# A gated group norm whose mean square and root are computed on all 128 partitions over the whole block, in place of column sums, a root on four columns, and diagonals

## The chip, the cores and the metric

The kernel runs on one core of one Trainium2 chip. The metric is the device time of one execution in microseconds. TensorE is called PE, VectorE DVE, ScalarE ACT, GpSimd POOL, and SyncE, which issues most of the transfers, SP.

## The reference

One layer of a hybrid decoder trunk over T = 2112 tokens (2048 of a prompt, 64 of a sample group) of width 1024, all in float32. Three token mixers (a Mamba-2 scan, a convolution module, a causal pooling) are projected from the same normed input, gated and merged. What the change touches is the end of the Mamba branch:

```python
def rmsnorm(x, w):
    xf = x.astype(jnp.float32)
    y = xf * lax.rsqrt(jnp.mean(xf * xf, axis=-1, keepdims=True) + EPS)
    return (y * w.astype(jnp.float32)).astype(x.dtype)

def mamba_branch(z, xbc, dt_raw, ...):
    ...
    y, h_new = ssd_scan(xs, dt, a_log, bm, cm, h0)
    y = (y + d_skip[:, None].astype(y.dtype) * xs).reshape(bsz, L, D_SSM)
    yg = (y * jax.nn.silu(z)).reshape(bsz, L, SSM_GROUPS, D_SSM // SSM_GROUPS)
    yg = rmsnorm(yg, jnp.ones((D_SSM // SSM_GROUPS,), jnp.float32)).reshape(bsz, L, D_SSM)
    return yg * norm_w.astype(yg.dtype), new_buf, h_new
```

So the 1024 channels of `y * silu(z)` are divided by the root mean square of their group of 512 (two groups), one root for each token and group. `z` is a product of the normed input with 1024 columns of the input projection.

## The kernel before

Activations lie transposed, channels on the partitions and tokens along the free axis. The tokens are cut into five blocks, `TB`: 512, 512, 512, 256 and 320. Every float32 product of the projections is made of float16 halves: `mm3` issues, for each of the 8 slices of the contraction, three matmuls (24 in all, each of one block's tokens) that add into one PSUM tile `mm`, of which there are three in turn (`mmt`). PE's instructions keep the order in which the program writes them. The other engines' instructions are put in order by the framework's scheduler, which simulates the kernel; an engine then takes its instructions strictly in that order.

Work that goes beside the products is put into a list, `side`. After each matmul of `mm3` the list's clock moves on by n / 2400 us, and a step of the list whose time has come is written at that place. `z_norm` below is such a step: it comes 9.0 us of that clock behind its block.

The stage of the change is the z stage (lines 1234 to 1287 before): for each of the two channel groups `g`, and in it for the blocks in the order 256, 320, 512, 512, 512, `z_in` does four times (`cc`), for 128 channels each:

- SP loads `yg` (the scan's result, from DRAM, L1247 and L1249; eight buffers) and `xs` (L1252; two buffers), and DVE makes `yg + d * xs` in `yg` (L1253);
- PE makes the product of z, 24 matmuls (L365, tile `mm`);
- ACT takes its silu out of PSUM into `sz` (L1258; one buffer), which gives the `mm` tile back, and DVE multiplies `yg` by it (L1259);
- ACT squares `yg`, for the first `cc` into `sacc` (L1261; one buffer), for the others into `sz` (L1263), and DVE adds `sz` to `sacc` (L1264).

Then `z_norm`: for each 128 tokens a matmul of a block of `sacc` with one column of ones gives the sums over the partitions as a column (L1272, tile `pvz`, 128 x 1). `rstd_of` (L179 to L186) makes the inverse root of up to four such columns on DVE, by the integer first guess and three Newton steps, twelve instructions on 128 x 4. 7.0 us later `bcast_steps` spreads the root over the partitions again: for each 128 tokens DVE makes a diagonal (L197) and PE multiplies ones by it (L199, tile `rBz`). DVE multiplies the four `yg` by `rBz` (L1280), ACT and DVE make from each the two float16 halves `ya` (L1281, L1282), which later products of the output projection read.

Weights of later products are converted during the stage too: ACT (L228, L247) and DVE (L251, 128 x 1024, two in a row), with a small product for the scale (L136 on PE into an `mm` tile, read by L138 on DVE).

Of the kernel before, what the change touches and what calls it, by code (L numbers as in the profile page):

```python
# [11 lines left out]
F32 = mybir.dt.float32  # L12
F16 = mybir.dt.float16
BF16 = mybir.dt.bfloat16
I32 = mybir.dt.int32
AF = mybir.ActivationFunctionType
ALU = mybir.AluOpType
# [4 lines left out]
P = 128  # L22
# [9 lines left out]
EPS = 1e-6  # L32
# [10 lines left out]
def tiles_of(n):  # L43

    return [min(o, n - P) for o in range(0, n, P)]
# [7 lines left out]
def trunk_body(tc, I, O):  # L53
    nc = tc.nc
    V, S, G, PE, DMA = nc.vector, nc.scalar, nc.gpsimd, nc.tensor, nc.sync
    MUL, ADD, SUB, MAX = ALU.mult, ALU.add, ALU.subtract, ALU.max
# [36 lines left out]
    ident, tri, ones = cst[:, C_ID:C_ID + P], cst[:, C_TRI:C_TRI + P], cst[:, C_ONE:C_ONE + P]  # L93
# [77 lines left out]
    def rstd_of(ss, n, cnt, eng, name):  # L171

        r = ss.shape[0]

        def sm(nm, dt=F32):
            return smp.tile([P, 4], dt, name=nm, tag=f"rs_{nm}", bufs=4)[:r, :n]

        v, i1, y, a, b = sm("rv"), sm("ri", I32), sm("ry"), sm("ra"), sm("rb")
        V.tensor_scalar(v, ss, 1.0 / cnt, EPS, op0=MUL, op1=ADD)  # L179
        V.tensor_scalar(i1, v.bitcast(I32), 1, None, op0=ALU.logical_shift_right)  # L180
        V.tensor_scalar(y.bitcast(I32), i1, -1.0, float(0x5F3759DF), op0=MUL, op1=ADD)
        for it in range(3):
            eng.tensor_tensor(a, y, y, op=MUL)
            eng.scalar_tensor_tensor(b, a, -0.5, v, op0=MUL, op1=MUL)
            y2 = sm(f"ry{it}")
            eng.scalar_tensor_tensor(y2, b, 1.5, y, op0=ADD, op1=MUL)  # L186
            y = y2
        return y

    def bcast_steps(ps, cols, offs, pace=0.64):  # L190

        dgs = []
        for i, o in enumerate(offs):
            while len(dgs) < min(i + 3, len(offs)):
                q = len(dgs)
                dgs.append(smp.tile([P, P], F32, name="diag", tag="diag", bufs=3))
                V.tensor_scalar(dgs[q], ident, cols[:, q:q + 1], None, op0=MUL)  # L197
            yield pace
            PE.matmul(ps[:, o:o + P], ones, dgs[i], start=True, stop=True)  # L199
# [159 lines left out]
    side, wside = Side(), Side()  # L359
# [102 lines left out]
    start = tc.manual_schedule(engines={mybir.EngineType.DVE, mybir.EngineType.Activation, mybir.EngineType.SP})  # L462
# [766 lines left out]
    pps = pool("pps", 2, space=PSUM)  # L1229
    zps = pool("zps", 2, space=PSUM)  # L1230

    Z_GAPS = (9.0, 7.0)

    def z_in(g, bi, zw):

        t0, n = TB[bi]
        pn = PN[bi]
        sacc = zp.tile([P, 512], F32, name="sacc", tag="sacc")[:, :n]
        yg = []
        for cc in range(4):  # L1240
            k = 4 * g + cc

            o = n * (cc % 2) if 2 * n <= 512 else 0
            if o == 0:
                yt = zp.tile([P, 512], F32, name="yg", tag="yg", bufs=8)
            yk = yt[:, o:o + n]
            DMA.dma_start(out=yk[:, :pn].rearrange("p (i t) -> p i t", t=P), in_=y_d[t0 // P:(t0 + pn) // P, :, k].rearrange("i p t -> p i t"))  # L1247
            if pn < n:
                DMA.dma_start(out=yk[:, pn:], in_=y_d[NC, :, k, :TS])  # L1249
            yg.append(yk)  # L1250
            xs = zp.tile([P, 512], F32, name="xs", tag="xs", bufs=2)[:, :n]
            DMA.dma_start(out=xs, in_=xbc_d[k, :, t0:t0 + n])  # L1252
            V.scalar_tensor_tensor(yk, xs, dsk[:, k:k + 1], yk, op0=MUL, op1=ADD)  # L1253
            wz, iz = zw[cc // 2]
            pz = mmt(n)
            mm3(pz, wz, (cc % 2) * P, hT[bi], n)
            sz = zp.tile([P, 512], F32, name="sz", tag="sz", bufs=1)[:, :n]
            S.activation(sz, pz, AF.Silu, scale=iz)  # L1258
            V.tensor_tensor(yk, yk, sz, op=MUL)  # L1259
            if cc == 0:  # L1260
                S.activation(sacc, yk, AF.Square)  # L1261
            else:
                S.activation(sz, yk, AF.Square)  # L1263
                V.tensor_tensor(sacc, sacc, sz, op=ADD)  # L1264
        side.add(z_norm(g, bi, yg, sacc), Z_GAPS[0])

    def z_norm(g, bi, yg, sacc):
        n = TB[bi][1]
        offs = tiles_of(n)
        pv = zps.tile([P, 4], F32, name="pvz", tag="pvz", bufs=1)  # L1270
        for i, o in enumerate(offs):
            PE.matmul(pv[:, i:i + 1], sacc[:, o:o + P], ones[:, 0:1], start=True, stop=True)  # L1272
            yield 0.64
        rs = rstd_of(pv[:, :len(offs)], len(offs), 512, V, "z")
        yield Z_GAPS[1]
        rB = zps.tile([P, 512], F32, name="rBz", tag="rBz", bufs=2)
        yield from bcast_steps(rB, rs, offs)
        for cc in range(4):
            k = 4 * g + cc
            V.tensor_tensor(yg[cc], yg[cc], rB[:, :n], op=MUL)  # L1280
            S.activation(ya[bi][:, 0, k], yg[cc], AF.Copy, scale=snws[:, k:k + 1])  # L1281
            V.scalar_tensor_tensor(ya[bi][:, 1, k], yg[cc], snws[:, k:k + 1], ya[bi][:, 0, k], op0=MUL, op1=SUB)  # L1282

# [247 lines left out]
```

## Time and profile before

| | us |
|---|---|
| median of 3 runs | 2228.59 |
| lowest and highest | 2225.47, 2231.59 |
| profiled execution | 2221.09 |
| its span in the trace | 2219.0 |
| PE busy in it | 2148.2 (97%) |
| DVE busy | 1369.9 (62%) |
| ACT busy | 908.4 (41%) |
| POOL busy | 255.9 (12%) |

The profile comes from one execution, the 2221.09 us; the 2.1 us by which that is longer than the span lie outside it. Start times in the trace count from the span's start. "Busy" is the time in which the engine has an instruction in work; for PE overlapping matmuls count once. A float32 matmul leaves two records in the trace. [...]

### The profile page before, as it was taken

To read this page: it belongs to the slowest core of one execution; us is meant where nothing else is said; L and a number is where in the kernel's file an instruction comes from. 1 tells how busy PE (TensorE), PEld (TensorE's weight loads), DVE (VectorE), ACT (ScalarE), POOL (GpSimd) and SP (SyncE) were. 2 spreads that over 40 slices of the span, in tenths; PEclk is the share of its full clock that TensorE was granted. 3 is DMA by queue.
4 is the path that set the end of the run, shared out by engine and by line. 5 is a ranking of instruction groups with operands and counts; after the bars stand their busy time and mean duration, and the time that the engine had idled before them with its cause. 6 is when DMAs were issued, how large, how long until landed. Compare 5 with 4: busy or idle time off the path is not lost.

```text
span 2219.0 us, 33878 instructions
## 1 busy us (share of the span) xinstructions
PE 2148.2 (97%) x13188; PEld 1275.5 (57%) x13188; DVE 1369.9 (62%) x2414; ACT 908.4 (41%) x1647; POOL 255.9 (12%) x579
## 2 busy tenths in 40 slices
PE   5999999999999999999999999999999999999998
PEld 3565555555555565545555555556645555557886
DVE  6689888884777786889954443436676332233544
ACT  6431444458666564154343232224444222232222
POOL 0010111111111111132210011100000000001222
PEclk9999999999999999999999999999999999999999
DMA  7332221226665554452323233334241222236321
GB/s 267 119 88 74 74 88 69 88 90 208 171 152 167 166 151 149 157 180 84 111 84 99 73 114 116 116 107 143 83 130 62 90 91 66 74 109 208 115 101 44
DMA packets 203505, 259.57 MB, mean 117 GB/s; under 512 B 51409, under 2 KB 142161, under 8 KB 203345
## 3 DMA queue, kind: packets, MB, share of 16 engines
q1 hardware_dynamic: 184848, 218.89, 31.8%
q0 software_dynamic: 6896, 22.30, 2.9%
q10 hardware_dynamic: 11600, 16.22, 2.1%
q8 instruction: 103, 1.69, 0.3%
q14 instruction: 58, 0.47, 0.1%
HBM read 179.06 MB, written 78.30 MB: 116 GB/s over the span
## 4 chain that ended last, share of the span: by engine, by line
PE 67%; DVE 16%; DMA 6%; ACT 5%; issue 4%; POOL 1%; SPq 0%; DVEq 0%; POOLq 0%; ACTq 0%
PE mm L365 51%; DVE acc L665 6%; DVE ct L729 4%; PE po L1390 2%; PE po L1391 2%; PE po L1392 2%; PE y L843 2%; DMA R<-acT_d 1%; DVE w L251 1%; DMA xs<-xbc_d 1%; ACT w L247 1%; PE off L853 1%; ACT R L819 1%; PE st L861 1%; DMA c_d<-acc 1%
## 5 line engine op out<-in xcount | busy, mean ns | idle before, releaser
L365 PE MATMUL mm<-hT,w 128*128 128x512 f16 (+2 forms) x7728 | 1505.6, 342 | 18.1 <-ACT ue L716 6.4
L365 PEld LDWEIGHTS <-w 128*128 128x128 f16 x9696 | 944.4, 99 | 755.4 <-issue 85.4
L665 DVE SCALAR_TENSOR_TENSOR acc<-vx,vec,acc 128x512 f32<-128x512 f32 (+1 forms) x330 | 326.8, 990 | 6.8
L365 PE MATMUL mm<-ya,w 128*128 128x512 f16 (+2 forms) x888 | 161.9, 339 | 0.0
L247 ACT ACTIVATE w<-wst,sw 128x1024 f16<-128x1024 f32 x86 | 94.4, 1140 | 128.0 <-POOL sw L162 127.9
L1143 DVE SCALAR_TENSOR_TENSOR msg<-mm,mi,msg 128x512 f32<-128x512 f32 (+2 forms) x80 | 52.4, 655 | 152.2 <-PE mm L365 116.0
L1138 ACT ACTIVATE msg<-mm,winv 128x512 f32<-128x512 f32 (+2 forms) x80 | 48.7, 609 | 223.1 <-PE mm L365 221.7
L251 DVE SCALAR_TENSOR_TENSOR w<-wst,sw,w 128x1024 f16<-128x1024 f32 x86 | 107.4, 1280 | 46.0 <-ACT w L247 46.0
L228 ACT ACTIVATE w<-wst 128x1024 f16<-128x1024 f32 x86 | 90.3, 1052 | 105.2 <-DMA wst<-in_w_in 63.5
L1357 DVE SCALAR_TENSOR_TENSOR sg<-mm,winv,sg 128x512 f32<-128x512 f32 (+2 forms) x37 | 24.0, 649 | 156.6 <-PE mm L365 156.6
L729 DVE SCALAR_TENSOR_TENSOR ct<-ue,vec,ct 128x1024 f32<-128x1024 f32 (+1 forms) x108 | 101.6, 950 | 18.1 <-ACT ct L727 15.6
L158 POOL TENSOR_SCALAR pcw<-prw 128x1 f32<-128x1 f32 x49 | 20.7, 422 | 784.6 <-DVE prw L138 733.5
L819 ACT ACTIVATE R<-R,acum 128x128 f32<-128x128 f32 (+1 forms) x272 | 82.4, 385 | 55.3 <-DMA R<-acT_d 48.3
L1391 PE MATMUL po<-w,m 128*128 128x256 f16 x384 | 104.7, 273 | 0.0
L1390 PE MATMUL po<-w,m 128*128 128x256 f16 x384 | 104.7, 273 | 0.0
L1392 PE MATMUL po<-w,m 128*128 128x256 f16 x384 | 104.7, 273 | 0.0
L365 PE MATMUL mm<-yc,w 128*128 128x512 f16 (+2 forms) x480 | 92.3, 342 | 0.0
L365 PE MATMUL mm<-yb,w 128*128 128x512 f16 (+2 forms) x480 | 92.2, 342 | 0.0
L1406 DVE SCALAR_TENSOR_TENSOR xo<-po,winv,xo 128x256 f32<-128x256 f32 (+1 forms) x68 | 32.7, 482 | 72.2 <-PE po L1392 71.3
L1368 ACT ACTIVATE mt<-ml,msc 128x512 f16<-128x512 f32 (+2 forms) x35 | 22.6, 645 | 124.1 <-DVE ml L1358 116.2
L1408 ACT ACTIVATE jo<-xo 128x256 bf16<-128x256 f32 (+1 forms) x68 | 28.3, 416 | 101.0 <-DVE xo L1406 70.2
L1409 POOL TENSOR_TENSOR xo<-xo,fnw 128x256 f32<-128x256 f32 (+1 forms) x68 | 50.1, 738 | 157.2 <-ACT jo L1408 122.6
(300 smaller groups left out, 2427.5 us busy)
## 6 DMA issues: line engine op xcount, KB each, us to landing
wst<-in_w_in SPq DMA_DIRECT2D x64, 512.0 KB, 4.6
R<-acT_d SPq DMA_DIRECT2D x32, 512.0 KB, 4.6
xbc_d<-so SPq DMA_DIRECT2D x24, 512.0 KB, 2.7
m_d<-msg SPq DMA_DIRECT2D x48, 256.0 KB, 2.0
ml<-m_d SPq DMA_DIRECT2D x48, 256.0 KB, 2.9
xc<-xbc_d SPq DMA_DIRECT2D x32, 256.0 KB, 3.6
R<-acT_d SPq DMA_DIRECT2D x64, 128.0 KB, 3.1
y_d<-R POOLq DMA_DIRECT2D x32, 256.0 KB, 3.5
```

The lines of the kernel that those rows point to most:

```text
L228: S.activation(w[:, 0, ks], st, AF.Abs, accum_out=mk)
L247: S.activation(w[:, 0, ks], st, AF.Copy, scale=s)
L251: V.scalar_tensor_tensor(w[:, 1, ks], st, s, w[:, 0, ks], op0=MUL, op1=SUB)
L365: PE.matmul(ps, w[:, i, k, c0:c0 + cw_], a[:, j, k, a0:a0 + n], start=(q == 0), stop=(q == len(passes) - 1))
L665: V.scalar_tensor_tensor(acc, vt[:, j:j + n], fw[:, cb, j:j + 1], acc, op0=MUL, op1=ADD)
L729: V.scalar_tensor_tensor(dst, src[j], cw[:, cb, j:j + 1], dst, op0=MUL, op1=ADD)
L819: S.activation(R[:L, h], R[:L, h], AF.Relu, scale=-1.0, bias=acum[:L, col:col + 1])
L1143: V.scalar_tensor_tensor(sg, po, iv, sg, op0=MUL, op1=MUL)
L1390: PE.matmul(ps, mh, wt[:, 0, k], start=(k == 0), stop=False)
L1391: PE.matmul(ps, mh, wt[:, 1, k], start=False, stop=False)
L1392: PE.matmul(ps, ml_, wt[:, 0, k], start=False, stop=(k == KD - 1))
L1409: G.tensor_tensor(xs, xs, fnw[:w, c * 256:(c + 1) * 256], op=MUL)
```

## The change

The column sums, the root on four columns, the diagonals and their products go. One matmul per block multiplies a 128 x 128 tile of ones by the whole `sacc` (up to 128 x 512), so that every partition of the PSUM tile `pvz` holds the sums of all tokens. The twelve instructions of the root then run on DVE over the whole width, with `v` (mean plus epsilon) written over `sacc`, the guess `y` in a new tile `zy` (one buffer), and the intermediate products in `pvz` itself, in PSUM. The four `yg` are multiplied by `zy`.

```diff
-    Z_GAPS = (9.0, 7.0)
+    Z_GAP = 9.0
...
-        side.add(z_norm(g, bi, yg, sacc), Z_GAPS[0])
+        side.add(z_norm(g, bi, yg, sacc), Z_GAP)
 
     def z_norm(g, bi, yg, sacc):
+
         n = TB[bi][1]
-        offs = tiles_of(n)
-        pv = zps.tile([P, 4], F32, name="pvz", tag="pvz", bufs=1)
-        for i, o in enumerate(offs):
-            PE.matmul(pv[:, i:i + 1], sacc[:, o:o + P], ones[:, 0:1], start=True, stop=True)
-            yield 0.64
-        rs = rstd_of(pv[:, :len(offs)], len(offs), 512, V, "z")
-        yield Z_GAPS[1]
-        rB = zps.tile([P, 512], F32, name="rBz", tag="rBz", bufs=2)
-        yield from bcast_steps(rB, rs, offs)
+        pv = zps.tile([P, 512], F32, name="pvz", tag="pvz", bufs=2)[:, :n]
+        PE.matmul(pv, ones, sacc, start=True, stop=True)
+        yield 0.64
+        v = sacc
+        V.tensor_scalar(v, pv, 1.0 / 512, EPS, op0=MUL, op1=ADD)
+        y = zp.tile([P, 512], F32, name="zy", tag="zy", bufs=1)[:, :n]
+        V.tensor_scalar(y.bitcast(I32), v.bitcast(I32), 1, None, op0=ALU.logical_shift_right)
+        V.tensor_scalar(y.bitcast(I32), y.bitcast(I32), -1.0, float(0x5F3759DF), op0=MUL, op1=ADD)
+        for _ in range(3):
+            yield 2.0
+            V.tensor_tensor(pv, y, y, op=MUL)
+            V.scalar_tensor_tensor(pv, pv, -0.5, v, op0=MUL, op1=MUL)
+            V.scalar_tensor_tensor(y, pv, 1.5, y, op0=ADD, op1=MUL)
+        yield 2.0
         for cc in range(4):
             k = 4 * g + cc
-            V.tensor_tensor(yg[cc], yg[cc], rB[:, :n], op=MUL)
+            V.tensor_tensor(yg[cc], yg[cc], y, op=MUL)
```

In the lines of the kernel after, the ones product is L1271, the three instructions of the first guess L1274, L1276 and L1277, a Newton step L1280 to L1282, the multiplication of `yg` L1286, and the halves L1287 (ACT) and L1288 (DVE).

DVE, from the end of the first 512 block's root of the first channel group to just ahead of the next block's root. Before (`ry` and `diag` are the root and the diagonals):

```order
L186 SCALAR_TENSOR_TENSOR ry_14471<-rb,ry_14467 128x4
L197 TENSOR_SCALAR diag<-cst,ry_14471 128x128 x3
L1259 TENSOR_TENSOR yg<-yg,sz 128x512
L1264 TENSOR_TENSOR sacc<-sacc,sz 128x512
L197 TENSOR_SCALAR diag<-cst,ry_14471 128x128
L1259 TENSOR_TENSOR yg<-yg,sz 128x512
L1280 TENSOR_TENSOR yg<-yg,rBz 128x512 x4
L1264 TENSOR_TENSOR sacc<-sacc,sz 128x512
L1282 SCALAR_TENSOR_TENSOR ya_13781<-yg,snws,ya_13781 128x512 x4
L1253 SCALAR_TENSOR_TENSOR yg<-xs,vec,yg 128x512 x2
L1259 TENSOR_TENSOR yg<-yg,sz 128x512
L1253 SCALAR_TENSOR_TENSOR yg<-xs,vec,yg 128x512 x2
```

The same place after:

```order
L1282 SCALAR_TENSOR_TENSOR zy<-pvz,zy 128x512
L1264 TENSOR_TENSOR sacc<-sacc,sz 128x512
L1286 TENSOR_TENSOR yg<-yg,zy 128x512 x4
L1259 TENSOR_TENSOR yg<-yg,sz 128x512
L1288 SCALAR_TENSOR_TENSOR ya_13781<-yg,snws,ya_13781 128x512 x4
L1264 TENSOR_TENSOR sacc<-sacc,sz 128x512
L1253 SCALAR_TENSOR_TENSOR yg<-xs,vec,yg 128x512 x2
L1259 TENSOR_TENSOR yg<-yg,sz 128x512
L1253 SCALAR_TENSOR_TENSOR yg<-xs,vec,yg 128x512
L1264 TENSOR_TENSOR sacc<-sacc,sz 128x512
L1253 SCALAR_TENSOR_TENSOR yg<-xs,vec,yg 128x512
L1259 TENSOR_TENSOR yg<-yg,sz 128x512
```

All three additions to the current block's `sacc` (L1264) now stand behind the whole root of the block before it, and the last of them behind a third L1253, which is of the block after.

ACT, at the turn from the first channel group to the second, where the 256 block follows the last 512 block. Before:

```order
L1281 ACTIVATE ya_13782<-yg,snws 128x512 x4
L1258 ACTIVATE sz<-mm,winv 128x256 x2
L1263 ACTIVATE sz<-yg 128x256
L1261 ACTIVATE sacc<-yg 128x256
L1258 ACTIVATE sz<-mm,winv 128x256
L1263 ACTIVATE sz<-yg 128x256
L1258 ACTIVATE sz<-mm,winv 128x256
```

After:

```order
L1258 ACTIVATE sz<-mm,winv 128x256 x2
L1263 ACTIVATE sz<-yg 128x256
L1261 ACTIVATE sacc<-yg 128x256
L1258 ACTIVATE sz<-mm,winv 128x256
L1287 ACTIVATE ya_13783<-yg,snws 128x512 x4
L1263 ACTIVATE sz<-yg 128x256
L1258 ACTIVATE sz<-mm,winv 128x256
```

The place of L1261 in the row is the same, ahead of the silu of the third product (L1258); but the one buffer of `sacc`, into which it writes, is now read by the root of the block before until that root's last L1281, and the halves of that block (L1287) stand between the third silu and the fourth, where before they came much later.

## Rows read from the trace of the kernel before

**Rows 1.** The page, busy time of each engine.

```profile
PE 2148.2 (97%) x13188; PEld 1275.5 (57%) x13188; DVE 1369.9 (62%) x2414; ACT 908.4 (41%) x1647; POOL 255.9 (12%) x579
```

**Rows 2.** Windows: length; busy PE, PEld, DVE, ACT, POOL; PEclk; DMA; GB/s.

```profile
1494.60:1704.60 210.00, 205.31 (x1200) 120.73 (x1198) 140.35 (x362) 89.12 (x158) 5.67 (x25) 0.99 0.35 104
1600.00:1640.00 40.00, 36.00 (x204) 20.81 (x203) 31.27 (x90) 20.35 (x37) 2.44 (x10) 0.96 0.38 116
1704.60:2030.00 325.40, 325.40 (x1838) 179.28 (x1836) 103.95 (x155) 93.09 (x149) 8.31 (x40) 1.00 0.33 105
```

**Rows 3.** PE's waits in the z stage: total us, times, longest.

```profile
PE rBz L199 <- DVE diag L197: 3.2, 2, 2.8
```

**Rows 4.** Windows again, just behind that longest wait.

```profile
1620.60:1624.00 3.40, 3.39 (x11) 1.77 (x12) 1.37 (x4) 0.79 (x2) 0.00 (x0) 0.54 0.61 184
```

**Rows 5.** DVE groups in the z stage: count | busy, mean ns | idle before.

```profile
L1253 DVE SCALAR_TENSOR_TENSOR yg<-xs,vec,yg 128x512 f32<-128x512 f32 x24 | 17.9, 750 | 21.5 <-DMA xs<-xbc_d 10.8 <-DMA yg<-y_d 7.9 <-issue 2.2
L1259 DVE TENSOR_TENSOR yg<-yg,sz 128x512 f32<-128x512 f32 x24 | 16.5, 687 | 8.0 <-ACT sz L1258 8.0
...
L197 DVE TENSOR_SCALAR diag<-cst,ry 128x128 f32<-128x128 f32 x34 | 8.2, 283 | 5.3 <-PE rBz L199 4.9
L1253 DVE SCALAR_TENSOR_TENSOR yg<-xs,vec,yg 128x320 f32<-128x320 f32 x8 | 4.3, 550 | 4.7 <-DMA xs<-xbc_d 4.3 <-DMA yg<-y_d 0.5
...
L1253 DVE SCALAR_TENSOR_TENSOR yg<-xs,vec,yg 128x256 f32<-128x256 f32 x8 | 3.8, 484 | 6.1 <-DMA xs<-xbc_d 5.6 <-DMA yg<-y_d 0.5
...
L183 DVE TENSOR_TENSOR ra<-ry 128x4 f32<-128x4 f32 x18 | 2.9, 162 | 0.6
...
L1143 DVE SCALAR_TENSOR_TENSOR msg<-mm,mi,msg 128x320 f32<-128x320 f32 x1 | 0.6, 550 | 3.5 <-PE mm L365 3.5
```

**Rows 6.** PE's timeline: start, us, line, tiles, count [idle before <-releaser].

```profile
975.93 1.02 PE L1172 MATMUL pmu<-s,cst 128*128 128x512 f32 x2
976.79 3.62 PE L365 MATMUL mm<-hT,w 128*128 128x512 f16 x16
...
1514.78 0.28 PE L1272 MATMUL pvz<-cst,sacc 128*128 128x1 f32 x2
...
1551.44 0.28 PE L1272 MATMUL pvz<-cst,sacc 128*128 128x1 f32 x2
...
1573.59 0.28 PE L1272 MATMUL pvz<-cst,sacc 128*128 128x1 f32 x2
...
1704.61 15.70 PE L365 MATMUL gp<-ya,w 128*128 128x512 f16 x72
1720.15 1.04 PE L365 MATMUL mm<-ya,w 128*128 128x256 f16 x8
```

**Rows 7.** Timeline of DVE and SP's queue between two 512 blocks.

```profile
1568.39 2.73 DVE L1282 SCALAR_TENSOR_TENSOR ya<-yg,snws,ya 128x512 f16<-128x512 f32 x4
1572.12 0.75 DVE L1253 SCALAR_TENSOR_TENSOR yg<-xs,vec,yg 128x512 f32<-128x512 f32 x1 [1.00 <-DMA yg<-y_d]
...
1576.35 0.75 DVE L1253 SCALAR_TENSOR_TENSOR yg<-xs,vec,yg 128x512 f32<-128x512 f32 x1 [1.86 <-DMA xs<-xbc_d]
...
1569.16 2.35 SPq L1247 DMA_DIRECT2D yg<-y_d  x4
1572.90 5.26 SPq L1252 DMA_DIRECT2D xs<-xbc_d  x4
```

**Rows 8.** The tile `xs`: from issue to landing of its 40 loads.

```profile
DMA to landing us min/median/max: 2.1/2.6/4.4
```

**Rows 9.** Other wide DVE instructions: L662 (min/median/max ns); a run of L665.

```profile
L662 DVE TENSOR_SCALAR acc<-vx,vec x11: 539/546/812, 119.8 to 1080.6; 128x512 f32<-128x512 f32 x6, 128x1024 f32<-128x1024 f32 x5
...
1006.23 4.68 DVE L665 SCALAR_TENSOR_TENSOR acc<-vx,vec,acc 128x512 f32<-128x512 f32 x6
```

**Rows 10.** DVE's timeline ahead of the first root.

```profile
1517.05 2.48 DVE L251 SCALAR_TENSOR_TENSOR w<-wst,sw,w 128x1024 f16<-128x1024 f32 x2 [1.27 <-ACT w L247]
```

## The prediction, made before the changed kernel was run

> **What bounds the kernel now.** The page's busy times come first: PE works 2148.2 of 2219.0 us [rows 1], so a change counts as far as it changes what PE does or waits for. Next the windows by stage: in the z stage, 1494.6 to 1704.6, PE is busy 205.3 of 210.0 us, DVE 140.35, ACT 89.1; behind it PE has no gap up to 2030 [rows 2]. So PE sets the end of the stage with 4.7 us of idle time, and a microsecond lost or won there reaches the end of the kernel almost whole. Then the waits of PE: of the 4.7 us, 3.2 are for diagonals, 2.8 of it once [rows 3], in the window 1600 to 1640, at the turn of the channel groups, which holds 4.0 of the idle time [rows 2]. Behind that wait the clock was granted at 0.54 for 3.4 us, the half level [rows 4]: 3.4 x 0.46 = 1.6 us more. DVE has a third of the stage free, but not evenly: its L1253 already waits for loads, 21.5 us for the 512 blocks alone [rows 5].
>
> **PE's work.** Two column sums at 1551.44 and 1573.59 lie one 512 block apart, 22.15 us. The block's 96 matmuls take 96 x (1720.15 - 1704.61) / 72 = 20.72 us [rows 6]. The rest, 1.43 us, is four column sums and four diagonal products. There are 34 of each in the stage (the count of L197) [rows 5], so 34 / 4 x 1.43 = 12.2 us go. The nearest row for the new product is L1172, float32, 128 x 512, also two records: 976.79 - 975.93 = 0.86 us [rows 6]. In proportion to width it is 0.54 for 320 and 0.43 for 256; six, two and two of them make 7.1 us. PE's work falls by **5.1 us**, and a 512 block takes 20.72 + 0.86 = 21.58.
>
> **The root.** Twelve DVE instructions per block of 0.16 us (L183) [rows 5] become twelve at full width. At 512: three products at 0.687 (L1259), six three-operand ones at 0.75 (L1253) [rows 5], three scalar ones at 0.54 (L662) [rows 9]: 8.2 us. Each needs the one before; six such instructions in a row took 4.68 us, 0.78 each [rows 9], so with 0.03 to 0.04 between them a root takes **8.7 us**. By 484 against 750 ns [rows 5] it is 5.6 us at 256; at 320 by 550, 6.4. The scheduler also drops an L1259 or a reduction into some of them. Busy DVE in the stage: 140.35 - 120 x 0.16 - 34 x 0.283 + 6 x 8.2 + 2 x 6.0 + 2 x 5.3 = about 184 of 210. No row shows DVE writing PSUM, as L1280 and L1281 do. Instructions that read PSUM cost the same (L1143 at 320: 550 ns, L1253: 550 [rows 5]); I take no extra. The bounds are the distance between two kinds at one width, 0.06 us each way: 0.4 per root, 2.4 us on the six roots that lie on PE's path below.
>
> [...]
>
> [...]
>
> The diagonals' waits go (4.7 us of idle time and 1.6 us of clock). In their place three things queue behind the root.
>
> **Who waits for the root.** `v` lies in the one `sacc`. Until the last L1281 has read it, ACT's L1261 of the next block can't write there, and behind it on ACT stand the silus that give the `mm` tiles back; on DVE the L1264 of the next block stand behind all twelve. PE has three `mm` tiles and then stops.
>
> (a) The start. DVE has two weight conversions ahead of the first root until 1519.5 [rows 10]; before, twelve short instructions followed. Now 5.6 us of root, then one L1286, one L1264 and a silu, some 1.6 us, free the `mm` tile at 1526.7. PE reads `sacc` at 1514.8 as before [rows 6] and then has 0.43 + 28 x 0.135 (rest of the 320 block) + 24 x 0.216 = 9.4 us of work: 1524.2. **Wait 2.6.** Then 19 matmuls, 4.1 us, to the next ones product, whose `sacc` is complete 6.2 us later (L1288, two silus, L1259 and L1264 in turn): **wait 2.0**.
>
> (b) A 512 block behind a 512 block. From the start of a root to the next on DVE: 8.7, an L1259 and an L1264 (1.3), four L1286 (2.4, overlapping), an L1259 (0.65), the first L1288 (0.75): 13.8. That releases `yg` for a load: from the end of the first L1282 (1569.1) to its L1253 at 1572.12 it took 3.0 us; that L1253, 0.75, then releases `xs`, and the third L1253 stands 3.45 us behind (1572.9 to 1576.35) [rows 7]. It takes 0.75, and in the new order the last L1264 (0.65) stands behind it: 22.4. The ones product and the way to it add 1.1: **23.5 against PE's 21.58**, 1.9 us of wait. Before, the last L1264 didn't stand behind that load. This order holds for three of the block changes (320 to 512 in the first group, first to second 512 in both). For second to third in the first group the same walk gives 1.8. Together **7.5**.
>
> (c) The turn of the groups. The last 512 block's root (8.7) falls into the 256 block, where PE needs only 2.6 us per product. From the start of the ones product PE has 0.86 + 11 x 0.109 + 24 x 0.135 = 5.3 us until it needs the `mm` tile of the third product, whose silu waits for L1261. That comes at 0.9 (product) + 0.9 (DVE still at work) + 8.7 + 0.9 (L1264, silu) = 11.4: **wait 6.1**. After 14 matmuls (1.9 us) L136 needs the fourth product's tile. Its silu needs `sz`, so L1264, which stands behind four L1286 (2.4), L1259 (0.4) and four L1288 (2.8): **wait 4.0**, with L138 0.7. The 320 block behind meets the same pair in small, with its own weights' L251 before its root: **2.8 and 1.8**. Together 15.4. The last root is covered: its `ya` is read by the product behind the first one of 15.7 us [rows 6].
>
> The sum: -5.1 - 4.7 - 1.6 + 4.6 + 7.5 + 15.4 + 1.6 (I leave one fall of the clock at the turn, where the longest wait now is) = **+17.7 us**. The profiled execution would take 2221.1 + 17.7 = 2238.8; it lies 7.5 us under the median of the runs, so the median is forecast at 2228.6 + 17.7 = **2246**.
>
> Low end: 8.2 for a root (no gaps, six on the path, -3.0), `xs` landing at its median 2.6 [rows 8] with 0.3 to pick up (three times -0.55), no fall of the clock (-1.6), quicker PSUM writes (-1.5): +10. High end: dearer PSUM writes (+2.4), both loads at 4.4 [rows 8] in some changes (+3), two more falls (+3.2): +26.
>
> **Rivals.** *PE's work alone* (the other side). DVE is free for 26 us of the stage even with 184 busy. If the loads were there when DVE comes, (b) is 22.4 - 2 x 2.5 + 1.1 = 18.5, under PE's 21.58, and nothing waits; if the DVE's lead of a few us then carried over the turn, only (a) and a few us of (c) stay. It decides where the path of (b) is under 21.58 and DVE enters the turn with 6 us in hand. Then -11.4 + 2 to 11 = about -9 to 0: 2219 to 2229. For it: the stage's share of DVE is 88%, not 100%. Against it: L1253 waited for loads even before [rows 5], and the 5.3 us of cover at the turn is PE's own work, whatever DVE did earlier.
>
> *Half of it*: (b) or half of (c) fails to appear, the rest stands: 17.7 - 7.5 = +10, down to 17.7 - 15 = +3: 2232 to 2239. For it: PE's lag at each block gives DVE and the loads time that the walk counts block by block.
>
> *More falls and slower loads*: each wait of (a) and (c) of over 2 us brings the clock down as the 2.8 us did [rows 3, 4], five times 1.6 in place of one, and loads of 4.4: +26 to +35, 2255 to 2264. For it: the one long wait of before did so. Against: I see only one case.
> [...]
>
> That the change doesn't do what it says can be left out: the order of the instructions shows all twelve at full width.
>
> **How the numbers follow.** The forecast (+10 to +26, 2239 to 2255): 60 in 100. PE's work alone: 12, of which 9 are over 0.3% faster. Half of it: 16, of which 10 within 0.3% (6.7 us, about what a measurement of this kernel can tell from no change) and 6 over. More falls: 12. Slower: 60 + 6 + 12 = 78; same: 10 + 3 = 13; faster 9. The range leaves out most of the second case and some of the last: 2228 to 2261.
>
> **What would show it.** Length of the z stage (210.0 now) about 228; DVE busy in it 184; L1271 at 0.86 from start to start; L1280 to L1282 at 0.69 to 0.75 each; PE waits for ACT at L365 of 6 and 4 us behind the last ones product of the first group; 512 blocks 23.5 apart from ones product to ones product. I am wrong if the 512 blocks come 21.6 apart, if PE waits at the turn for under 5 us in all, or if PE loses time behind 1705 as well.

## The result and the profile after

The kernel after takes 2245.83 us (median of 4 runs, 2242.34 to 2247.99), the kernel before beside it 2227.03 (2222.70 to 2231.59): a ratio of 1.0083 with a 95% interval of 1.0057 to 1.0109, or 12.7 to 24.3 us more. The forecast was 17.7 us more.

The page of the kernel after, busy time of each engine [rows 1]:

```profile
PE 2148.2 (96%) x13072; PEld 1264.1 (56%) x13072; DVE 1411.4 (63%) x2380; ACT 908.2 (40%) x1647; POOL 255.6 (11%) x579
```

PE's busy time has not moved at all, although it has 116 records less. DVE has 41.5 us more work in 34 instructions less.

The profiled execution of after is 2247.99 us long, 26.9 us more than that of before. Part of this has nothing to do with the change: up to the first ones product PE's instructions are the same one for one (DVE's up to the first root, ACT's up to the first square of the 320 block), and after is 6.4 us late there already (the L136 product starts at 1517.20, before at 1510.81; the experiments below, with the same instructions up to there, reach it between 1508.7 and 1517.6). So the stage is measured in both from that L136 to the first product behind the stage (`gp`), over the same work. Windows (length; busy PE, PEld, DVE, ACT, POOL; PEclk, the granted TensorE clock as a share of full speed; DMA; GB/s) of before and then of after:

```profile
1510.81:1704.61 193.80, 189.10 (x1063) 107.24 (x1061) 132.32 (x343) 82.51 (x144) 5.67 (x25) 0.99 0.32 97
```

```profile
1517.20:1731.34 214.14, 189.00 (x946) 95.18 (x944) 173.74 (x311) 82.29 (x143) 5.51 (x25) 0.96 0.30 89
1536.00:1540.00 4.00, 4.00 (x13) 1.47 (x12) 3.10 (x8) 2.24 (x6) 0.00 (x0) 0.66 0.26 75
1624.80:1628.40 3.60, 3.34 (x14) 1.83 (x14) 3.60 (x7) 2.84 (x5) 0.00 (x0) 0.63 0.00 0
1631.00:1635.00 4.00, 4.00 (x19) 2.42 (x18) 1.65 (x5) 2.36 (x4) 1.18 (x5) 0.59 0.83 247
1648.00:1652.00 4.00, 3.81 (x11) 1.46 (x11) 3.35 (x9) 2.33 (x6) 0.00 (x0) 0.58 0.22 65
```

The stage is 20.3 us longer. PE idles in it 214.14 - 189.00 = 25.1 us, where it idled 4.7. It is busy as long as before in spite of less work: in four stretches the clock stands at 0.58 to 0.66, and the same instructions at a clock of 1.00 take 182.1 us (e5 below). So 6.9 us of its busy time is clock, where before had 1.6 by the prediction's estimate. Behind the stage nothing more is lost: from the `gp` product to the end it is 2245.8 - 1731.34 = 514.5 us, before 2219.0 - 1704.61 = 514.4.

PE's waits in the stage (in total, times, longest), and then its timeline, of which only the rows with a wait in brackets and the ones product at the turn stand here:

```profile
PE mm L365 <- ACT sz L1258: 15.1, 4, 7.4
PE pvz L1271 <- DVE sacc L1264: 7.7, 5, 2.6
PE mm L136 <- ACT sz L1258: 2.3, 1, 2.3
```

```profile
1519.83 2.88 PE L365 MATMUL mm<-hT,w 128*128 128x320 f16 x20 [1.60 <-ACT sz L1258]
...
1535.88 5.65 PE L365 MATMUL mm<-hT,w 128*128 128x512 f16 x19 [3.76 <-ACT sz L1258]
1542.72 0.81 PE L1271 MATMUL pvz<-sacc,cst 128*128 128x320 f32 x2 [1.20 <-DVE sacc L1264]
...
1566.86 1.12 PE L1271 MATMUL pvz<-sacc,cst 128*128 128x512 f32 x2 [2.55 <-DVE sacc L1264]
...
1590.05 1.13 PE L1271 MATMUL pvz<-sacc,cst 128*128 128x512 f32 x2 [1.34 <-DVE sacc L1264]
...
1611.92 1.02 PE L1271 MATMUL pvz<-sacc,cst 128*128 128x512 f32 x2
1612.78 4.62 PE L365 MATMUL mm<-hT,w 128*128 128x256 f16 x35
1624.78 3.36 PE L365 MATMUL mm<-hT,w 128*128 128x320 f16 x14 [7.37 <-ACT sz L1258]
1630.49 0.22 PE L136 MATMUL mm<-dgm,ones 128*128 128x128 bf16 x1 [2.34 <-ACT sz L1258]
...
1648.19 5.81 PE L365 MATMUL mm<-hT,w 128*128 128x512 f16 x19 [2.32 <-ACT sz L1258]
1655.12 0.81 PE L1271 MATMUL pvz<-sacc,cst 128*128 128x320 f32 x2 [1.12 <-DVE sacc L1264]
...
1699.81 1.12 PE L1271 MATMUL pvz<-sacc,cst 128*128 128x512 f32 x2 [1.53 <-DVE sacc L1264]
```

They stand where the prediction put them: the start, the changes between 512 blocks, the turn and the small blocks behind it. The first, of 1.60 us, stands ahead of everything that was changed. The rows of the turn show the hold on `sacc` at work. DVE's root of the last 512 block, ACT's square into the same `sacc`, and the silu behind it, here DVE and then ACT (timeline: start, us, line, tiles, count, [idle before <- releaser]):

```profile
1614.18 0.55 DVE L1253 SCALAR_TENSOR_TENSOR yg<-xs,vec,yg 128x320 f32<-128x320 f32 x1 [1.19 <-DMA xs<-xbc_d]
1615.15 0.55 DVE L1253 SCALAR_TENSOR_TENSOR yg<-xs,vec,yg 128x320 f32<-128x320 f32 x1 [0.42 <-DMA xs<-xbc_d]
1615.62 0.68 DVE L1274 TENSOR_SCALAR sacc<-pvz 128x512 f32<-128x512 f32 x1
...
1623.12 0.69 DVE L1282 SCALAR_TENSOR_TENSOR zy<-pvz,zy 128x512 f32<-128x512 f32 x1
1623.72 0.41 DVE L1264 TENSOR_TENSOR sacc<-sacc,sz 128x256 f32<-128x256 f32 x1
```

```profile
1623.12 0.42 ACT L1261 ACTIVATE sacc<-yg 128x256 f32<-128x256 f32 x1 [9.68 <-DVE pvz L1281]
1624.26 0.47 ACT L1258 ACTIVATE sz<-mm,winv 128x256 f32<-128x256 f32 x1 [0.72 <-DVE sacc L1264]
```

ACT stands 9.7 us in front of L1261 until the last L1281 has read `v`; one addition and one silu later, at 1624.78, PE goes on.

At the start (and behind the turn, where a 320 block again follows a 256 block) something comes on top that the prediction does not have. Here is the end of the 256 block's reading of `v` on DVE, then ACT:

```profile
1531.76 0.43 DVE L1281 SCALAR_TENSOR_TENSOR pvz<-pvz,sacc 128x256 f32<-128x256 f32 x1
```

```profile
1530.07 1.06 ACT L228 ACTIVATE w<-wst 128x1024 f16<-128x1024 f32 x1 [3.70 <-DMA wst<-in_w_in]
...
1532.41 1.06 ACT L228 ACTIVATE w<-wst 128x1024 f16<-128x1024 f32 x1 [1.19 <-DMA wst<-in_w_in]
...
1534.23 0.45 ACT L1261 ACTIVATE sacc<-yg 128x320 f32<-128x320 f32 x1
```

`v` has been read at 1532.2, but L1261 runs at 1534.2: two weight conversions (L228), which wait for the load of their weight, stand ahead of it. In the kernel before they stand behind it:

```profile
1518.33 0.45 ACT L1261 ACTIVATE sacc<-yg 128x320 f32<-128x320 f32 x1
...
1522.09 1.06 ACT L228 ACTIVATE w<-wst 128x1024 f16<-128x1024 f32 x1 [1.53 <-DMA wst<-in_w_in]
```

In the second group it is the same (`v` read at 1644.1, L1261 at 1646.5). With L1261 right behind the last L1281, the addition on DVE could have followed the first L1286, which ends at 1533.1 and 1645.0, and the silu that PE waits for could have come 1.6 and 2.1 us sooner. So about 1.6 us of the wait of 3.8, and 2.1 of the 2.3 at 1648.19, are ACT's new order and not the root's length; this is worked out from the rows and was not tried. In all runs in which `v` holds `sacc` (after, e1, e3, e6, e7) one or both L228 stand ahead of the first 320 block's L1261; with `sacc` free after the product (before, e2, e4, e5, e8, e9) they stand behind it. So the order goes with the hold, by way of the scheduler.

### The profile page after: what moved, and what is told of

Its sections match the earlier page's. It is cut to its first block, busy times and chain, and to the rows that moved or that the text cites. A ratio compares the mean times of both kernels' runs of the same rounds, so it can differ in the third digit from the quotient of the medians.

```text
span 2245.8 us, 33603 instructions
## 1 busy us (share of the span) xinstructions
PE 2148.2 (96%) x13072; PEld 1264.1 (56%) x13072; DVE 1411.4 (63%) x2380; ACT 908.2 (40%) x1647; POOL 255.6 (11%) x579
## 4 chain that ended last, share of the span: by engine, by line
PE 54%; DVE 17%; DMA 8%; issue 5%; ACT 3%; POOL 1%; SPq 0%; DVEq 0%; POOLq 0%; ACTq 0%
PE mm L365 40%; DVE acc L665 6%; DVE ct L729 4%; PE po L1396 2%; PE po L1398 2%; PE po L1397 2%; DMA xs<-xbc_d 2%; DMA R<-acT_d 2%; PE y L843 2%; DVE w L251 1%; DMA yg<-y_d 1%; DMA c_d<-acc 1%; PE off L853 1%; ACT w L247 1%; PE st L861 1%
## 5 line engine op out<-in xcount | busy, mean ns | idle before, releaser
L665 DVE SCALAR_TENSOR_TENSOR acc<-vx,vec,acc 128x512 f32<-128x512 f32 (+1 forms) x330 | 326.9, 990 | 6.8
L1143 DVE SCALAR_TENSOR_TENSOR msg<-mm,mi,msg 128x512 f32<-128x512 f32 (+2 forms) x80 | 52.4, 655 | 152.0 <-PE mm L365 115.4
L251 DVE SCALAR_TENSOR_TENSOR w<-wst,sw,w 128x1024 f16<-128x1024 f32 x86 | 107.5, 1280 | 44.7 <-ACT w L247 44.7
L228 ACT ACTIVATE w<-wst 128x1024 f16<-128x1024 f32 x86 | 90.2, 1051 | 109.3 <-DMA wst<-in_w_in 68.3
L843 PE MATMUL y<-R,xd 128*64 128x128 f32 (+1 forms) x544 | 60.4, 301 | 8.1 <-DVE R L856 8.0
```

The source lines that it names most:

```text
L228: S.activation(w[:, 0, ks], st, AF.Abs, accum_out=mk)
L251: V.scalar_tensor_tensor(w[:, 1, ks], st, s, w[:, 0, ks], op0=MUL, op1=SUB)
L665: V.scalar_tensor_tensor(acc, vt[:, j:j + n], fw[:, cb, j:j + 1], acc, op0=MUL, op1=ADD)
L843: PE.matmul(py[hh * 64:(hh + 1) * 64, b], xd[:L, 2 * b + hh], R[:L, 2 * b + hh], start=True, stop=True)
L1143: V.scalar_tensor_tensor(sg, po, iv, sg, op0=MUL, op1=MUL)
```

## The experiments

"Stage" below is the length from the L136 product to the first `gp` product, as above (before 193.8, after 214.1). Ratios are to runs of the kernel before on the same chip. A stage is read from one profile each. How well it repeats is seen in e7, whose engines have the instructions of after, in the same order, until past the second 512 block's ones product of the first group:

```profile
1580.98 1.12 PE L1271 MATMUL pvz<-sacc,cst 128*128 128x512 f32 x2 [0.85 <-DVE sacc L1264]
```

From L136 to there it takes 1580.98 - 1511.39 = 69.6 us, after 1590.05 - 1517.20 = 72.9. So two profiles of the same work can differ by 3 us, and a difference of stages of that size shows nothing by itself.

### e1: the root on four columns

It leaves out the root of all but four tokens of a block (the other columns of the factor are a constant).

```diff
+    zy0 = zp.tile([P, 512], F32, name="zy", tag="zy", bufs=1)
+    G.memset(zy0, 1.0)
...
-        v = sacc
+        v = sacc[:, :4]
+        pw = pv
+        pv = pw[:, :4]
...
-        y = zp.tile([P, 512], F32, name="zy", tag="zy", bufs=1)[:, :n]
+        yw = zy0[:, :n]
+        y = yw[:, :4]
...
-            V.tensor_tensor(yg[cc], yg[cc], y, op=MUL)
+            V.tensor_tensor(yg[cc], yg[cc], yw, op=MUL)
```

> The kernel after, but the twelve instructions of the root work on the first 4 columns only and the other columns of the factor are a constant; it leaves out the root of all other tokens and keeps the ones product, the hold on sacc and all places in the program. If the loss comes from the length of the root (8.7 us at 512 where twelve short ones took about 2.4), PE's waits of the z stage (25.1 us in the kernel after) fall to under 3 us, no clock falls there, and only the change of PE's own work is left, -5.1, with the 4.7 us of waits and 1.6 us of clock of before gone as well: 9 to 11 us under the kernel before (ratio 0.995 to 0.996). If the loss comes from the wide float32 product itself, from the clock or from the new order alone, it stays within 5 us of the kernel after (ratio 1.006 to 1.010).

Ratio 1.0001 (0.9991 to 1.0010). The stage is 194.4 us, 19.7 less than after: with a root on four columns nearly the whole loss is gone. But the gain of 9 to 11 us over before did not come. The window of the stage and PE's waits in it:

```profile
1514.92:1709.31 194.39, 182.07 (x947) 93.48 (x944) 132.17 (x317) 85.61 (x150) 7.44 (x23) 1.00 0.33 101
```

```profile
PE mm L365 <- ACT sz L1260: 7.0, 4, 2.7
PE mm L136 <- ACT sz L1260: 2.8, 1, 2.8
PE pvz L1273 <- DVE sacc L1266: 2.5, 2, 1.3
```

PE's work is down as forecast, 182.1 us at full clock. What it wins is given back in 12.3 us of waits, though the root takes 2.4 us now. Two of them, of 2.75 and 2.81 us, have no fall of the clock behind them (PEclk is 1.00 over the stage). (The silu is L1260 here, the addition L1266.)

### e2: the same wide root, but `sacc` free

```diff
-        v = sacc
+        v = pv
...
+        t = zps.tile([P, 512], F32, name="zt", tag="zt", bufs=1)[:, :n]
...
-            V.tensor_tensor(pv, y, y, op=MUL)
-            V.scalar_tensor_tensor(pv, pv, -0.5, v, op0=MUL, op1=MUL)
-            V.scalar_tensor_tensor(y, pv, 1.5, y, op0=ADD, op1=MUL)
+            V.tensor_tensor(t, v, y, op=MUL)
+            V.scalar_tensor_tensor(t, t, -0.5, y, op0=MUL, op1=MUL)
+            V.scalar_tensor_tensor(y, t, 1.5, y, op0=ADD, op1=MUL)
```

> The kernel after with v left in PSUM in place of sacc, and the Newton product in a second PSUM tile (t = v*y, t = -0.5*t*y, y = (t+1.5)*y): the same twelve instructions at the same width, but sacc is free once the ones product has read it. If the hold on sacc is the path, as I think, the waits for the silu at the start and at the turn go (3.8 + 1.6 + 7.4 + 2.3 + 2.3 us of the kernel after, and most of its 6 us of half-level clock); DVE's busy time in the stage stays at about 184 us: 4 us under to 5 us over the kernel before (0.998 to 1.002). If it is DVE's time alone (the next block's additions behind twelve wide instructions on an engine in order), the time stays at +15 to +20 us (1.007 to 1.009).

Ratio 1.0043 (1.0026 to 1.0060), or 9.6 us over before; the stage is 200.1 us, 14.1 less than after and 6.3 over before. (The profiled execution, 2225.08 us, is the fastest of the four; their median is 2231.36.) It falls between the two theories:

```profile
1508.68:1708.74 200.06, 186.80 (x947) 94.74 (x945) 169.74 (x309) 81.40 (x143) 6.51 (x25) 0.97 0.31 94
```

```profile
PE pvz L1271 <- DVE sacc L1264: 10.4, 3, 6.2
PE mm L365 <- ACT sz L1258: 2.4, 2, 2.0
PE mm L136 <- ACT sz L1258: 0.4, 1, 0.4
```

DVE does as much as in after (169.7 us against 173.7), and the silus' waits are down from 17.4 to 2.8. In their place PE waits for the last additions to `sacc`, 3.9 and 6.2 us at the ones products of a 512 and of the second 320 block. Freeing `sacc` also let the scheduler put the additions between the instructions of the root, so this run changes the order on DVE along with the hold.

### e3: two Newton steps in place of three

```diff
-        for _ in range(3):
+        for _ in range(2):
```

> The kernel after with two Newton steps in place of three, nothing else: a root at 512 is 3 instructions, 2.2 us, shorter. If each wait is the end of a root that PE has run into, every wait behind a root shortens by the root's own saving until it is zero: 3.8 to 2.4, 1.2 to 0, 2.6 to 0.4, 1.3 to 0, 7.4 to 5.2, 2.3 to 0.9, 1.5 to 0, about 11 us, with 1 us less of half-level clock: 8 us over the kernel before (1.003 to 1.005). If the waits are set by loads or by ACT, it stays near the kernel after (1.007 to 1.009).

It leaves out the third step. Ratio 1.0034 (1.0022 to 1.0046), or 7.6 us; the stage is 200.8 us, 7.0 over before, where 8 were expected. The sum came out, the single waits didn't. Of after's waits between 512 blocks 0.55 us is left, where about 0.4 was expected: those are the root's length. Of the 7.4 us one 2.55 is left, where 5.2 were expected. The small blocks' waits did not shrink to 2.4 and 0.9 but are 4.3 and 2.7 us: there the rival, ACT, holds. At the start the last L1281 has read `v` at 1524.2, but L1261 runs at 1526.8, behind the two L228, and the silu at 1529.2, behind four halves. The clock fell behind four waits of 2.2 to 4.3 us (0.59 to 0.62), so that PE's busy time is still 188.5 us. The idle time came down by 12.8 us, the clock gave back 0.5.

### e4: a square root on ACT and a reciprocal on DVE

```diff
+    epsc = cp.tile([P, 1], F32, name="epsc")
+    G.memset(epsc, EPS)
...
+        S.activation(y, pv, AF.Sqrt, scale=1.0 / 512, bias=epsc)
+        V.reciprocal(y, y)
```

(in place of the twelve instructions)

> The kernel after with the root made by one square root on ACT (out of PSUM, with the scale and epsilon) and one reciprocal on DVE, in place of twelve DVE instructions. By the theory of the long root the DVE part shrinks from 8.7 us to about 1, PE's waits in the stage go as in the narrow root, and the time is 5 to 11 us under the kernel before (0.995 to 0.998). The rival is a new wait on ACT: a square root needs another function table than the silu, so two loads of a table and the root itself stand in ACT's queue in front of the silus that give PE its PSUM tiles; with two times over 1 us a block that would leave the time within 5 us of before or above it (0.999 to 1.003).

It also frees `sacc`, which nothing reads behind the ones product. Ratio 1.0019 (1.0009 to 1.0030): inside the rival's range, not the theory's; the stage is 196.6 us. Two rows of ACT's groups in the stage, and DVE's row at the turn:

```profile
L1276 ACT ACT_TABLE_LOAD x10 | 12.8, 1283 | 0.1
L1260 ACT ACT_TABLE_LOAD x9 | 11.5, 1283 | 0.2
```

```profile
1600.52 3.35 DVE L1277 RECIPROCAL zy<-zy 128x512 f32<-128x512 f32 x1 [1.57 <-ACT zy L1276]
```

Nineteen loads of a function table, 1.28 us each, stand in ACT's queue, and the reciprocal that was to take 1 us, an estimate from no row, takes 3.35. The silu of 1607.25 (L1260 here), for which PE's L136 waits 3.4 us, stands on ACT behind two loads of a table, the root, a square that had waited 1.9 us for DVE, where the reciprocal stood in front, and four halves. What the loads and what the long reciprocal cost was not tried apart.

### e5: both, a short root and a free `sacc`

e1 with `v` in a small tile of its own; it leaves out the same as e1.

```diff
-        v = sacc[:, :4]
+        v = smp.tile([P, 4], F32, name="zv", tag="zv", bufs=2)
```

> The narrow root of e1 (it leaves out the root of all but four tokens of a block), with v in a small tile of its own, so that sacc is free as soon as the ones product is read. e1 kept 12.3 us of PE's waits in the z stage with DVE almost as free as before. If these are the hold on sacc (ACT's square into sacc waits for the root, and the silu behind it), most of them go: 6 to 10 us under e1 and under the kernel before (ratio 0.995 to 0.998). If they are ACT's and DVE's new order, in which a block's halves stand ahead of the next silus, they stay within 4 us of e1 (0.999 to 1.001).

Ratio 0.9978 (0.9966 to 0.9989). The stage is 187.4 us, 7.0 under e1; waits fall from 12.3 to 5.3:

```profile
1512.32:1699.75 187.43, 182.06 (x946) 93.32 (x944) 130.30 (x318) 85.26 (x150) 8.82 (x23) 1.00 0.35 105
```

So what e1 kept was for the larger part the hold, even with a root of 2.4 us, together with the order that the scheduler makes of it: in e1 L1261 of the 320 block stands behind an L228 that waits 3.7 us for its load, in e5 ahead of both. What the waiting and what the order cost was not tried apart. With e1, e2 and after this makes a table of the stage, against before's 193.8:

| | `sacc` free | `sacc` held by `v` |
|---|---|---|
| root on 4 columns | e5: -6.4 | e1: +0.6 |
| root at full width | e2: +6.3 | after: +20.3 |

In these profiles the hold alone costs 7.0, the width alone 12.6, both together 26.7, 7.1 more than their sum. By the timed runs (e5 -4.9, e1 +0.2, e2 +9.6, after +18.5) it is 5.1, 14.5 and 23.4, an excess of 3.8 with four intervals of 2 to 6 us either way. That each of the two costs something is clear of these intervals; that a hold is the dearer, the longer the thing that holds, is not.

### e6: without the loads of `xs`

It leaves out the 40 loads (L1253 reads one tile that is loaded once).

```diff
+    xs0 = zp.tile([P, 512], F32, name="xs", tag="xs", bufs=1)
+    DMA.dma_start(out=xs0, in_=xbc_d[0, :, :512])
...
-            xs = zp.tile([P, 512], F32, name="xs", tag="xs", bufs=2)[:, :n]
-            DMA.dma_start(out=xs, in_=xbc_d[k, :, t0:t0 + n])
+            xs = xs0[:, :n]
```

> The kernel after without the 40 loads of xs: L1253 reads one tile that is loaded once (it leaves out the loads, so the sum takes wrong values). If a 512 block's path goes through the loads (root, halves, load of yg, load of xs, last addition), PE's waits for sacc between 512 blocks (2.6, 1.3 and 1.5 us) go and the root at the turn starts about 1.6 us sooner: the z stage is 7 to 9 us shorter than in the kernel after, 205 to 207 us from L136 to the first product behind the stage, where after has 214.1 and before 193.8. If DVE's own work is the path there, the stage stays at 212 to 215.

The stage is 205.6 us, 8.5 less than after: the expected sum, but not from the expected places. Between 512 blocks PE still waits 2.4, 0.8 and 0.4 us, 3.6 in place of 5.4. The rest came from the small blocks and the turn: 4.7 us in place of 7.4 there, 1.0 in place of 2.3 behind it, 0.7 in place of 3.8 at the start (the ones products of the two 320 blocks then wait 2.7 and 2.6 in place of 1.2 and 1.1), and PE's busy time is 186.5 in place of 189.0 with fewer falls of the clock. A wait of 1.1 us for a silu ahead of the turn is new. This rests on one profile and not on timed runs, and some of it is not the loads: up to the second 512 block's ones product e6 takes 67.5 us, after 72.9, but e7, with the loads, 69.6. The queues also had less to carry (55 GB/s in the stage in place of 89, a busy share of 0.18 in place of 0.30); what that did to the other loads was not read. With that said, the loads are on the path, in this profile more at the turn than between the 512 blocks.

### e7: the second group in the order 512, 512, 512, 256, 320

```diff
-        for bi in (3, 4, 0, 1, 2):
+        for bi in ((3, 4, 0, 1, 2), (0, 1, 2, 3, 4))[g]:
```

> The kernel after with the second channel group in the order 512, 512, 512, 256, 320 in place of 256, 320, 512, 512, 512; the same work. If the waits at the turn (7.4 and 2.3 us in the kernel after, with two stretches of half clock behind them) come from a 256 block behind a 512 block's root, there is no wait over 2 us for a silu where the groups meet, since PE then has 17 us of work under the root in place of 5.3, and the pair of waits, 6 to 8 and 2 to 4 us, stands at the second group's 512 to 256 change instead, 65 us later. If they come from the change of weights or from the groups themselves, they stay where they are.

The long wait moved with the 512 to 256 change (one profile, as in e6). Three rows of PE's timeline, at the groups' meeting and at that change:

```profile
1631.06 1.63 PE L1271 MATMUL pvz<-sacc,cst 128*128 128x512 f32 x2 [4.79 <-DVE sacc L1264]
...
1658.00 1.26 PE L1271 MATMUL pvz<-sacc,cst 128*128 128x512 f32 x2 [3.35 <-DVE sacc L1264]
...
1694.59 8.69 PE L365 MATMUL mm<-hT,w 128*128 128x320 f16 x44 [7.49 <-ACT sz L1258]
```

7.5 us for the silu, as at the turn before (7.4), and none for a silu where the groups meet. The second of the pair is missing; no L136 stands there. At the meeting PE waits 4.8 and 3.4 us for additions: two weight conversions (L251, 1.28 us each) stand among them on DVE each time, behind a root of 512. The stage is 215.4 us: the waits went elsewhere, not away.

### e8 and e9: a free `sacc` and two steps, and a later ones product

e8 is e2 and e3 together; e9 is e8 with

```diff
-    Z_GAP = 9.0
+    Z_GAP = 11.0
```

> e2 with two Newton steps in place of three: sacc free after the ones product, and a root 2.2 us shorter. e2 and e3 each took about two thirds of the loss; if hold and length are two terms that add, PE's waits of the stage fall from e2's 13.2 us to about 6 and the time is 1 us over to 6 us under the kernel before (0.997 to 1.001). If what e2 left (waits for the last additions to sacc, 3.9 and 6.2 us) comes from DVE's order and not from the root's length, it stays at e2's 1.003 to 1.005.

> e8 with the ones product written 11.0 in place of 9.0 us behind its block. e8's waits that are left are for the last addition to sacc at the ones product (5.3 us, 3.1 at most) and one silu (1.6). If the ones product is only placed too early for DVE, 2 us more take away most of the 5.3, at the price of a later root: 2 to 5 us under e8 (ratio to before 0.996 to 0.998). If the later root only moves the wait to the silus, since sacc is then free 2 us later, it stays at e8's 0.998 to 1.000.

e8: ratio 0.9984 (0.9972 to 0.9996), stage 190.7 us, waits 6.9 (7.1 by the window's idle time). e9: ratio 0.9980 (0.9971 to 0.9989), stage 188.6 us. Both are faster than both kernels; by the step's formula two steps leave a relative error of some 5e-6 (the guess's 3.4% becomes 0.18%, then 4.7e-6; the error of a step is 1.5 times the square of the one before). The window of e9:

```profile
1513.51:1702.09 188.58, 181.86 (x947) 93.60 (x945) 154.29 (x279) 81.22 (x142) 6.30 (x25) 1.00 0.33 100
```

The clock is whole and PE's busy time is down to 181.9 us. e9's stage is 2.1 us shorter than e8's in one profile each; by their intervals the two can't be told apart. The waits did not move as expected: those for the additions fell from 5.3 to 4.3 us only, those for silus rose from 1.6 to 2.4. What e9's profile won is clock.

### e10: the kernel before with a later spreading of the root

```diff
-    Z_GAPS = (9.0, 7.0)
+    Z_GAPS = (9.0, 9.5)
```

> The kernel before with the diagonal products written 9.5 in place of 7.0 us behind the column sums, nothing else. Its largest wait is one of 2.8 us for a diagonal, with 1.6 us of half-level clock behind it. If that wait is all that the old form loses, the time falls by 3 to 5 us (ratio 0.998 to 0.999), and the gain of e8 over before is in part only this wait. If the later spreading runs into the next block's work, it stays at 0.999 to 1.002.

Ratio 1.0000 (0.9988 to 1.0011). The wait for the diagonal is gone, and one of 4.6 us for the last addition to `sacc`, at the column sums of the 320 block, has come in its place:

```profile
PE pvz L1272 <- DVE sacc L1264: 4.6, 1, 4.6
```

So the old form did not lose its 2.8 us through its spacing alone.

## Why the prediction was right, point by point

The forecast of +17.7 us came out at +18.8 (median). The mechanism was right: PE's work fell as forecast, the root holds `sacc` and DVE, and PE waits at the forecast places. That the sum is so close is in part luck, as the terms show, compared on the stage, +20.3:

| term, change against before | forecast | measured |
|---|---|---|
| PE's work | -5.1 | -5.4 (182.1 against 189.1 - 1.6, the 1.6 an estimate) |
| PE's idle time | +22.8 (27.5 - 4.7) | +20.4 (25.1 - 4.7) |
| clock | 0.0 (1.6 - 1.6) | +5.3 (6.9 - 1.6) |
| sum | +17.7 | +20.3 |

**PE's work.** The ones product is 1612.78 - 1611.92 = 0.86 us from start to start, the row of L1172 [rows 6] to the digit.

**The root.** At the turn it took 1615.62 to 1623.81, 8.2 us in place of 8.7: the two integer instructions take 0.43 us and not L662's 0.54 [rows 9], and the three-operand ones 0.69 and not 0.75 [rows 5]. DVE's busy time between the same points rose by 41.4 us, forecast 44. Groups of DVE in the stage of after:

```profile
L1280 DVE TENSOR_TENSOR pvz<-zy 128x512 f32<-128x512 f32 x18 | 12.6, 700 | 0.5
L1281 DVE SCALAR_TENSOR_TENSOR pvz<-pvz,sacc 128x512 f32<-128x512 f32 x18 | 12.5, 697 | 0.4
...
L1274 DVE TENSOR_SCALAR sacc<-pvz 128x512 f32<-128x512 f32 x6 | 4.1, 684 | 2.9 <-PE pvz L1271 2.9
...
L1277 DVE TENSOR_SCALAR zy<-zy 128x512 int32<-128x512 int32 x6 | 2.6, 427 | 0.2
```

Writing PSUM (L1280 0.700, L1281 0.697, beside L1259's 0.687 and L1282's 0.691) costs no more than 0.01 to 0.02 us, inside the bounds of 0.06. L1274, whose source is in PSUM, takes 0.684 and not the 0.54 of L662 [rows 9], whose source is a tile that a load filled; L1277, which has constants like L1274, but integers in SBUF, takes 0.43. What makes L1274 the longer was not tried alone. In the three-operand instructions a source in PSUM shows no cost: L1281 (0.697) and L1282 (0.691) are no longer than the product L1259 (0.687), which reads SBUF, by more than 0.01.

**(a) The start.** Forecast 2.6 and 2.0, measured 3.8 and 1.2. The sum holds, but not by the forecast's walk alone: this has the silu 1.6 us behind the root, where it came 3.2 us behind it, because ACT's two L228 stood between the root and L1261 (see the rows above). The 1.6 us wait ahead of the first ones product stands in front of all that was changed, and counts in the 20.4 all the same.

**(b) 512 behind 512.** Forecast 1.9 three times and 1.8; measured 2.6, 1.3 and 1.5, and none between second and third of the first group. The chain is as described where the last L1264 stands behind the third L1253: between the first and the second 512 block the ones products lie 1590.05 - 1566.86 = 23.2 us apart, in the second group 23.3, forecast 23.5. Between second and third of the first group it is 1611.92 - 1590.05 = 21.9: there the third L1253 (1610.74) comes behind the last L1264 (1609.19), so that the addition doesn't wait for that load, and the same walk did not hold. e3 shows that the root is in the chain: with 2.2 us less of it 0.55 us of the 5.4 is left. What e6 corrects is the weight of the loads: without those of `xs` two thirds of these waits stay in its one profile.

**(c) The turn.** Forecast 6.1, 4.0, 0.7, 2.8 and 1.8, in all 15.4; measured 7.4, 2.3, 2.3 and 1.1, in all 13.2. The first is longer because the root began 2.8 us behind the end of the ones product, not 0.9: two L1253 of the 320 block, which stand ahead of it on DVE, waited 1.2 and 0.4 us for `xs`. The rest is shorter. e2 shows that the hold makes the first pair: with `sacc` free it is 2.0 and 0.4 in place of 7.4 and 2.3, under a root as wide. e7 shows that the long wait belongs to the 512 to 256 change. In the pair behind it 2.1 of the 2.3 is ACT's order, as at the start.

**The clock** is the term that was mis-sized: one fall of 1.6 us was left in the sum, and PE lost 6.9. The rival of more falls had it at five times 1.6 and named the waits of over 2 us. The windows show a clock near half behind the waits for silus of 3.8, 7.4 and 2.3 us (0.66, 0.63 and 0.58), and behind L136's 2.3 (0.59). Behind the 2.6 us wait for the ones product at 1566.86 it stayed whole:

```profile
1567.00:1571.00 4.00, 4.00 (x17) 1.72 (x18) 3.75 (x7) 1.27 (x2) 0.00 (x0) 1.00 0.48 133
```

So the forecast's sum is close in part because idle time too large by 2.4 us (4 without the 1.6 us wait that isn't of the change) stood against a clock too small by 5.3. That is luck: nothing makes the one error cancel the other. Nor is every wait of over 2 us followed by a fall, as that rival has it. In the stages of all the profiles here the 14 waits of 3.1 us and more have a stretch of lower clock behind them: four of them were read as windows (0.56 to 0.66), behind the others the same products take longer (behind e8's 3.1 us the ones product takes 1.74 us, in after, behind 2.6 us and at a clock of 1.00, 1.12). Behind seven of the 15 between 2.0 and 2.9 us there is one too (0.54 to 0.62 in the six windows read), and behind eight there is none (a clock of 1.00 behind the one in after and e6's 2.05 us, and over the stages of e1 and e9, which have three; products of the usual length behind e6's 2.65 and 2.42 us and e7's 2.08).

**The rival of PE's work alone** was priced at -9 to 0 if DVE came in time. e1 shows that a short root isn't enough for it: with the hold on `sacc` the kernel is level with before. It takes both (e5: -6.4 in the stage), and that is less than the 11.4 us that were free to win, since 5.3 us of waits remain.

## What to carry to other kernels

Work taken off the bounding engine and handed to one that is a third idle costs nothing only if no one waits for the second engine in between: look for the single buffer that the longer step now holds, and follow who writes it next and what stands behind that writer in its queue. Look also at what the scheduler then puts in front of that writer. Here the same twelve wide instructions cost 20 us against before with `v` in the accumulator and 6 us with `v` left in PSUM (by the stage; 18.5 and 9.6 by the timed runs), and with a step less as well the change turned into a gain of 0.2%. When a sum has waits of several microseconds on TensorE in it, price the clock behind each of them too: in after four stretches at 0.58 to 0.66 of the clock cost 6.9 us.

## What was not expected of the hardware

- A float32 reciprocal on DVE of 128 x 512 took 3.35 us, as long as five of the other wide instructions of 0.68 to 0.75 (e4); at 256 columns 1.74.
- Three-operand instructions with constant scalars, on PSUM operands, took 0.69 to 0.70 us at 512 columns (L1281, L1282), those with a scalar column from SBUF 0.75 (L1253). A source in PSUM doesn't show as the difference: L1143, with a source in PSUM and a scalar column, takes 0.55 at 320 columns like L1253 [rows 5], L1281 with constants 0.50. That leaves the scalar column, which was not tried alone.
- Of the five waits of PE between 2.3 and 7.4 us in after, four were followed by a stretch near the half clock (0.58 to 0.66); the fifth, of 2.6 us, was not (1.00). In e1 waits of 2.75 and 2.81 us and in e9 one of 2.70 were not either (1.00 over both stages), in e3 one of 2.22 was (0.60).
